# Gate weights of one layer, part of them prepared early beside w_down

## The chip, the cores and the metric

The kernel runs on one core of a Trainium2 chip. The metric is device time in microseconds, the median of several runs. The core's engines each take instructions in their own order: TensorE (PE) for matmuls and transposes, VectorE (DVE), ScalarE (ACT), GpSimd (POOL) and SyncE (SP), which only issues DMAs. GpSimd can issue DMAs too.

## The reference, cut to what matters

One layer for 1,056 tokens (1,024 of a prompt and 32 of a sample) of width 1,024: attention and a gated recurrence in two branches, their mix through w_out, a feed-forward part with a convolution of three tokens, and an input of the layer through a gate. The end, which the change touches:

```python
    ffn = (jax.nn.gelu(ac, approximate=True) * u) @ w_down      # 2816 -> 1024
    x = x + _rms_norm(ffn, g_post_ffn)
    conv_tail = ap[:, ap.shape[1] - (CONV_W - 1):]

    x = x + (pe @ w_ple) * jax.nn.sigmoid(x @ w_ple_gate)       # 1024 -> 1024
    return x, new_k, new_v, s_fin.astype(x.dtype), conv_tail
```

All values are float32.

## The kernel before

A float32 product is made of three matmuls. Each operand is split into a high part, its cast to the matmul's own rounding (fp32r), and a low part, the operand less the high part; the matmuls are high by high, high by low and low by high. The cast is an ACT instruction and the subtraction a DVE instruction (L181 and L184 for plain weights), so each weight tile costs one of both.

The layer's products run one after the other, activations held with features on partitions and tokens along the row. w_up runs as a Strassen-Winograd scheme (L1665 to L1667). Then comes w_down: three groups g of 352 tokens, for each two halves q of 512 output columns, for each half 11 steps of 256 rows of the weight, so 66 steps of 24 matmuls. A step's raw weight (`wr`, 512 KB, two buffers) is loaded by SP, cast to `wh` and split to `wl`; `wh`, `wl` and the gate's parts share one ring of eight tiles (`wb`). After a half, `d_out` copies four banks to `acc`, and sums squares for the norm. `x2_start`, `x2_rows` and `x2_part` finish the norm of a group: sums over partitions and a reciprocal square root on DVE (L211 to L217), transposes of its result into rows on PE (L301), and then `acc` = `acc` times gain times row plus x (L1822, L1823), for each of eight column blocks. For the last group, g = 2, this happens inside the gate stage.

The gate product x @ w_ple_gate comes last. Token groups 0 and 1 are made together by four `gate_unit`s, each with seven products of a Strassen-Winograd scheme, n = 0 to 27, of 12 matmuls each (L2045, L2047, L2048); token group 2 is made by eight plain blocks of 24 matmuls (L200 to L202). The left factors of a unit are seven parts: three quarters of that unit's weight (each 512 rows by 128 columns, 256 KB) and four sums of quarters. Before, SP loads 16 quarters into five buffers (L1885); the four sums of the first unit are made by DVE and those of the other three by GpSimd (L1908 to L1915); every part is then cast by ACT and split by DVE (L1898, L1899). `gate_prepare(n + 3)` asks for parts three products ahead. The right factors, sums of `acc`, are made by `gate_ops` in w_down's last group, with `um` as a buffer.

Behind a product, DVE combines banks into y (L2061 to L2073, U2 and s1c and nU3 in `um`); `y_out` takes tanh on ACT (L1992), multiplies by the loaded `ple` term (L1993, DVE) and adds `acc` (L1994: GpSimd for the gate units, DVE for the plain blocks); `y_done` turns y round by three transposes on PE (L2007), copies it and stores it. `late` holds back y_done until two products later.

The order of instructions on each engine is set when the program is built, by a scheduler that goes by its own estimates of when things are ready; the order of the code is its starting point, and `behind(E)` makes what is in it come after the last instruction written so far for that engine. On the chip each engine and each queue of DMAs goes through its instructions in that order, and a wait holds up what stands behind it.

## Time and profile before

| | |
|---|---|
| median of three runs | 2016.76 us (2016.23 to 2016.99) |
| profiled execution | 2018.78 us, span 2016.6 us |
| mean granted PE clock | 0.997 |
| PE, DVE, ACT, POOL busy | 98%, 73%, 49%, 13% of the span |
| w_down on PE | 1646.5 to 1901.2 us |
| gate units on PE | 1901.4 to 1976.3 us |
| plain blocks on PE | 1976.6 to 2010.2 us |
| HBM traffic | 181.75 MB read, 65.32 MB written |

A row of groups in the profile gives line, engine, operation, written tile <- read tiles, shape and count, then busy time and mean of one in ns, then the idle time of the engine just before and what ended it. A row of waits gives the engine and line that waited, what it waited for, and total, times and longest in us. A row of windows gives the stretch, its length, then busy us and count for PE, its weight loads (PEld), DVE, ACT and POOL, the granted clock, the DMA engines' busy share and GB/s.

### The profile page before, as it was taken

What the parts mean: (1) busy time and instruction counts of PE and PEld (TensorE: products, weight loads), DVE (VectorE), ACT (ScalarE), POOL (GpSimd) and SP (SyncE); (2) the same over time, 40 slices, a digit from 0 to 9 for tenths busy, and PEclk for the clock granted to TensorE, in tenths of its full rate; (3) what the DMA queues carried; (4) which work ended last, traced back from release to release, by engine and by line L of the source; (5) the groups of instructions that cost most, each with busy time, mean ns of one, the idle gap of its engine ahead of it and who ended that gap; (6) DMA issues with size and microseconds to landing.
All of it is one profiled execution on the core that took longest, in us unless ns stands there. A gap on an engine that the chain in (4) does not pass through costs nothing. (4 is left out here: it accounts for less than half of the span.)

```text
span 2016.6 us, 37464 instructions
## 1 busy us (share of the span) xinstructions
PE 1979.0 (98%) x14234; PEld 1946.8 (97%) x14234; DVE 1479.0 (73%) x3249; ACT 985.5 (49%) x2220; POOL 261.8 (13%) x346
## 2 busy tenths in 40 slices
PE   7999999999999999999999999999999999999988
PEld 6999999999999999999999999999999999999988
DVE  6788888688888888553555878787878784647794
ACT  6555566566666666441224663333333344445453
POOL 2110100000000000002001113333333300000140
PEclk9999999999999999999999999999999999999999
DMA  8322311411111111486558572222222255565355
GB/s 265 101 87 82 104 59 53 155 43 58 57 38 53 37 53 53 135 248 205 170 177 275 196 249 84 65 91 69 86 75 80 79 169 199 201 211 180 103 153 151
DMA packets 259257, 249.52 MB, mean 124 GB/s; under 512 B 13621, under 2 KB 227144, under 8 KB 259077
## 3 DMA queue, kind: packets, MB, share of 16 engines
q1 hardware_dynamic: 250533, 219.12, 34.6%
q0 software_dynamic: 8464, 27.94, 3.9%
q8 instruction: 112, 1.84, 0.4%
q14 instruction: 68, 0.56, 0.1%
q10 hardware_dynamic: 80, 0.07, 0.0%
HBM read 181.75 MB, written 65.32 MB: 123 GB/s over the span
## 5 line engine op out<-in xcount | busy, mean ns | idle before, releaser
L1665 PE MATMUL st<-op,wt 128*128 128x264 f32 x1232 | 348.7, 283 | 4.1 <-ACT ple L1420 2.3
L1667 PE MATMUL st<-op,wt 128*128 128x264 f32 x1232 | 350.0, 284 | 0.0
L1666 PE MATMUL st<-op,wt 128*128 128x264 f32 x1232 | 348.2, 283 | 0.0
L184 DVE TENSOR_TENSOR wl<-wr,wh 128x1024 fp32r<-128x1024 f32 x132 | 162.2, 1229 | 118.6 <-ACT wh L181 110.8
L1665 PEld LDWEIGHTS st<-op,wt 128*128 128x128 f32 x1232 | 231.2, 188 | 5.2 <-ACT ple L1420 2.5
L1666 PEld LDWEIGHTS st<-op,wt 128*128 128x128 f32 x1232 | 231.6, 188 | 0.0
L1667 PEld LDWEIGHTS st<-op,wt 128*128 128x128 f32 x1232 | 231.0, 188 | 0.0
L181 ACT CAST wh<-wr 128x1024 fp32r<-128x1024 f32 x116 | 121.8, 1050 | 205.4 <-PE mm L201 135.7
L200 PE MATMUL mm<-ac,wh 128*128 128x352 f32 x528 | 171.0, 324 | 1.7 <-ACT sq L1802 0.9
L1444 ACT CAST wt<-wu 128x512 fp32r<-128x512 f32 x126 | 77.6, 618 | 188.5 <-POOL ab L1651 93.7
L201 PE MATMUL mm<-ac,wh 128*128 128x352 f32 x528 | 169.3, 321 | 0.0
L202 PE MATMUL mm<-ac,wl 128*128 128x352 f32 x528 | 169.2, 321 | 0.0
L200 PE MATMUL mm<-La,wh 128*128 128x384 f32 (+1 forms) x504 | 166.9, 332 | 0.3 <-ACT kt L340 0.3
L201 PE MATMUL mm<-Lb,wh 128*128 128x384 f32 (+1 forms) x504 | 162.8, 323 | 0.0
L202 PE MATMUL mm<-La,wl 128*128 128x384 f32 (+1 forms) x504 | 162.7, 323 | 0.0
L200 PE MATMUL mm<-Ra,wh 128*128 128x264 f32 x512 | 145.7, 285 | 0.0
L201 PE MATMUL mm<-Rb,wh 128*128 128x264 f32 x512 | 145.2, 284 | 0.0
L202 PE MATMUL mm<-Ra,wl 128*128 128x264 f32 x512 | 145.2, 284 | 0.0
L1445 DVE TENSOR_TENSOR wt<-wu,wt 128x512 fp32r<-128x512 f32 x126 | 101.2, 806 | 39.7 <-ACT wt L1444 39.7
L453 ACT ACTIVATE sc<-sc,st 128x257 f32<-128x257 f32 (+1 forms) x144 | 69.7, 485 | 74.9 <-DVE st L448 73.7
L200 PEld LDWEIGHTS mm<-ac,wh 128*128 128x128 f32 x528 | 99.2, 188 | 2.3 <-ACT sq L1802 1.2
L201 PEld LDWEIGHTS mm<-ac,wh 128*128 128x128 f32 x528 | 99.4, 188 | 0.0
(508 smaller groups left out, 5820.3 us busy)
## 6 DMA issues: line engine op xcount, KB each, us to landing
wr<-in_w_down_dram SPq DMA_DIRECT2D x66, 512.0 KB
wu<-in_w_up_dram SPq DMA_DIRECT2D x42, 512.0 KB
wu<-in_w_in_dram SPq DMA_DIRECT2D x32, 512.0 KB
wr<-in_w_in_dram SPq DMA_DIRECT2D x26, 512.0 KB
ac<-act_d SPq DMA_DIRECT2D x66, 176.0 KB
act_d<-Up SPq DMA_DIRECT2D x21, 528.0 KB
wr<-in_w_out_dram SPq DMA_DIRECT2D x16, 512.0 KB
pw_d<-pw POOLq DMA_DIRECT2D x11, 512.0 KB, 5.0
```

The source lines that it names most:

```text
L181: S.copy(hi[:], raw[:])
L184: V.tensor_tensor(lo[:], raw[:], hi[:].bitcast(F32), op=ALU.subtract)
L200: E.matmul(ps, wh, a, start=first and n == 0, stop=False)
L201: E.matmul(ps, wh, b, start=False, stop=False)
L202: E.matmul(ps, wl, a, start=False, stop=last and n == len(ks) - 1)
L453: S.activation(sc[:m_, h, b0:e_ + 1], sc[:m_, h, b0:e_ + 1], AF.Exp, bias=st[:m_, 0, h:h + 1], scale=-1.0, accum_out=st[:m_, 1, h:h + 1])
L1444: S.copy(t[:, 0], src)
L1445: V.tensor_tensor(t[:, 1], src, t[:, 0].bitcast(F32), op=ALU.subtract)
L1665: E.matmul(o, wh, xh, start=first and k == 0, stop=False, skip_group_check=True)
L1666: E.matmul(o, wh, xl, start=False, stop=False, skip_group_check=True)
L1667: E.matmul(o, wl, xh, start=False, stop=k == 3, skip_group_check=True)
```

## The change

A new generator, `gate_early`, is stepped while w_down runs. GpSimd's queue loads the four quarters of a unit into four buffers that are free then: two thirds of `um`, the buffer `wr5` (loaded later, in `gate_first`, before), and two tiles `we` of the ring for outputs. For the first unit, all seven parts are made there, one after the other through a single further tile `we` (`pw`): cast on ACT, store of the high part to DRAM (`pg_d`), subtraction in place on DVE, store of the low part. For the other three units only the sums are made, on DVE, in place, and stored to DRAM (`gs_d`). GpSimd issues these 16 loads and 26 stores of 256 KB.

In the gate stage the first unit's parts are then read from `pg_d`, high and low together, 512 KB each; for the other units `raw_load` reads nine quarters and twelve sums, and cast and split stay there. The y add of L1994 is on DVE for all. GpSimd has no arithmetic there any more. `gate_prepare` asks for four products ahead, `x2_rows(2)` comes at n = 5 behind PE's last instruction instead of at n = 3, `x2_part` at each odd n above 6 behind DVE's last instead of at each n above 4, and `y_done` three products later instead of two, behind PE's last instruction.

```diff
--- before.py
+++ after.py
@@ -124,6 +124,8 @@
     ple_d = dp.tile([P, 8, T], F32, name="ple_d")
     pc_d = [dp.tile([P, 2, 2, H], F32, name=f"pc_d{g}") for g in range(4)]
     act_d = [dp.tile([P, T], F32, name=f"act_d{f}") for f in range(NF)]
+    pg_d = [dp.tile([P, 2, 4, P], F32, name=f"pg_d{i}") for i in range(7)]
+    gs_d = [[dp.tile([P, 4, P], F32, name=f"gs_d{u}_{i}") for i in range(7)] for u in range(4)]
...
@@ -1877,61 +1879,77 @@
 
     quarters, gate_w = [], []
 
-    def quarter_load(n):
-        if n >= 16:
+    def quarter(u, j):
+
+        return rows_cols(w_ple_gate, (j % 2) * 4 * P, (2 * u + j // 2) * P, P, 4)[0]
+
+    extra = ep.tile([P, 4, P], F32R, name="wr5")
+
+    def gate_early():
+        bufs = [um[:, 0:2, :].rearrange("p a c -> p (a c)")[:, 0:512], extra[:].bitcast(F32)]
+        for _ in range(2):
+            t = ep.tile([P, 3, 256], F32, tag="yr", name=nm("we"), bufs=3)
+            bufs.append(t[:].rearrange("p a c -> p (a c)")[:, 0:512])
+        bufs = [b if len(b.shape) == 3 else b.rearrange("p (k c) -> p k c", k=4) for b in bufs]
+        pw = ep.tile([P, 3, 256], F32R, tag="yr", name=nm("we"), bufs=3)
+        pw = pw[:].rearrange("p a c -> p (a c)")[:, 0:512].rearrange("p (k c) -> p k c", k=4)
+        a11, a12, a21, a22 = bufs
+
+        def part(i, src):
+            S.copy(pw, src)
+            gdma(pg_d[i][:, 0], pw.bitcast(F32))
+            V.tensor_tensor(pw, src, pw.bitcast(F32), op=ALU.subtract)
+            gdma(pg_d[i][:, 1], pw.bitcast(F32))
+
+        for u in range(4):
+            for j, b in enumerate(bufs):
+                gdma(b, quarter(u, j))
+            yield
+            if u == 0:
+                for i, b in ((0, a11), (2, a12), (5, a22)):
+                    part(i, b)
+                    yield
+            for o, a, b in ((a22, a21, a22), (a21, a11, a21), (a11, a11, a22), (a12, a12, a11)):
+                V.tensor_tensor(o, a, b, op=ALU.add)
+            if u == 0:
+                for i, b in ((1, a11), (3, a21), (4, a22), (6, a12)):
+                    part(i, b)
+                    yield
+                continue
+            for i, b in ((1, a11), (3, a21), (4, a22), (6, a12)):
+                gdma(gs_d[u][i], b)
+            yield
+
+    def raw_load(n):
+
+        if n >= 28:
             return
-        u, j = divmod(n, 4)
-        c, k0 = ((2 * u, 0), (2 * u + 1, 0), (2 * u + 1, 4), (2 * u, 4))[j]
-        dma(quarters[n % 5], rows_cols(w_ple_gate, k0 * P, c * P, P, 4)[0])
+        u, i = divmod(n, 7)
+        j = {0: 0, 2: 1, 5: 3}.get(i)
+        dma(quarters[n % 5], quarter(u, j) if j is not None else gs_d[u][i])
 
     def gate_first():
         for _ in range(2):
             t = wp.tile([P, 2, 4, P], F32, tag="wr", name=nm("wr"), bufs=2)
             quarters.extend(t[:, i] for i in range(2))
-        quarters.append(ep.tile([P, 4, P], F32, name="wr5")[:])
-        for n in range(5):
-            quarter_load(n)
-
-    def gate_parts():
-        def parts(src):
-            t = part_tile()
-            S.copy(t[:, 0], src)
-            V.tensor_tensor(t[:, 1], src, t[:, 0].bitcast(F32), op=ALU.subtract)
-            gate_w.append(t)
-
-        for u in range(4):
-            n = 4 * u
-            a11, a21, a22, a12 = (quarters[(n + i) % 5] for i in range(4))
-            s1 = wp.tile([P, 4, P], F32, tag="wb", name=nm("sa"), bufs=8)[:]
-            adder = V if u == 0 else G
-            parts(a11)
-            adder.tensor_tensor(s1, a21, a22, op=ALU.add)
-            adder.tensor_tensor(a21, a11, a21, op=ALU.add)
-            adder.tensor_tensor(a11, a11, s1, op=ALU.add)
-            yield
-            parts(a11)
-            yield
-            parts(a12)
-            adder.tensor_tensor(a12, a12, a11, op=ALU.add)
-            quarter_load(n + 5)
-            yield
-            parts(a21)
-            quarter_load(n + 6)
-            yield
-            parts(s1)
-            yield
-            parts(a22)
-            quarter_load(n + 7)
-            yield
-            parts(a12)
-            quarter_load(n + 8)
-            yield
-
-    gate_gen, op_gen = gate_parts(), gate_ops()
+        quarters.append(extra[:].bitcast(F32))
+        for n in range(7, 12):
+            raw_load(n)
 
     def gate_prepare(n):
         while len(gate_w) < min(n + 1, 28):
-            next(gate_gen)
+            i = len(gate_w)
+            t = part_tile()
+            if i < 7:
+                dma(t[:].bitcast(F32), pg_d[i][:])
+            else:
+                src = quarters[i % 5]
+                S.copy(t[:, 0], src)
+                V.tensor_tensor(t[:, 1], src, t[:, 0].bitcast(F32), op=ALU.subtract)
+                raw_load(i + 5)
+            gate_w.append(t)
+
+    op_gen, early_gen = gate_ops(), gate_early()
 
...
@@ -1967,9 +1985,12 @@
                     op_steps({18: 1, 20: 1}.get(k, 0) if q == 0 else
                              {0: 1, 2: 2, 4: 1, 6: 1, 8: 1, 12: 1, 14: 2, 16: 1, 18: 1, 20: 1}.get(k, 0))
                     if q and k == 18:
+                        gate_prepare(2)
+                    if q and k == 20:
                         gate_first()
-                    if q and k == 20:
-                        gate_prepare(3)
+                        gate_prepare(4)
+                if g == 1:
+                    next(early_gen, None)
 
...
@@ -1981,7 +2002,6 @@
 
     def y_out(g, c, b, y=None):
 
-        adder = V if y is None else G
...
@@ -1991,7 +2011,7 @@
         for z_ in cols:
             S.activation(y[:, z_], b[:, z_], AF.Tanh, scale=0.5)
             V.scalar_tensor_tensor(y[:, z_], y[:, z_], 1.0, pl[:, z_], op0=ALU.add, op1=ALU.mult)
-            adder.tensor_tensor(y[:, z_], y[:, z_], a[:, z_], op=ALU.add)
+            V.tensor_tensor(y[:, z_], y[:, z_], a[:, z_], op=ALU.add)
         return y
 
...
@@ -2034,7 +2054,7 @@
         for i, (t, first) in enumerate(((x, True), (y, True), (x, False), (y, False), (zz, True),
                                         (y, False), (zz, False))):
             n = 7 * u + i
-            gate_prepare(n + 3)
+            gate_prepare(n + 4)
...
@@ -2048,10 +2068,12 @@
                 E.matmul(t, w[:, 1, k, :], a, start=False, stop=k == 3, skip_group_check=True)
             if n == 1:
                 x2_start(2)
-            if n == 3:
-                x2_rows(2)
-            if n > 4:
-                x2_part()
+            if n == 5:
+                with behind(E):
+                    x2_rows(2)
+            if n > 6 and n % 2:
+                with behind(V):
+                    x2_part()
...
@@ -2072,8 +2094,9 @@
             else:
                 V.tensor_tensor(r, U2, zz, op=ALU.add)
                 late.append((n, 1, c, y_out(1, c, r, r)))
-            while late and late[0][0] + 2 <= n:
-                y_done(*late.pop(0)[1:])
+            while late and late[0][0] + 3 <= n:
+                with behind(E):
+                    y_done(*late.pop(0)[1:])
 
```

Line numbers from there on are larger by two in the changed kernel, and by some twenty from `y_out` on: L181, L301, L1796 and L1994 before are L183, L303, L1798 and L2014 after.

ScalarE in w_down's first group, before: casts of weights (`wh`), one of an activation pair (`ac`), and the first copies of a finished half.

```order
L181 CAST wh_20182<-wr_20180 128x1024
L1756 CAST ac_19998<-ac_19999 128x704
L181 CAST wh_20212<-wr_20210 128x1024
L181 CAST wh_20242<-wr_20240 128x1024
L181 CAST wh_20272<-wr_20270 128x1024
L181 CAST wh_20302<-wr_20300 128x1024
L181 CAST wh_20332<-wr_20330 128x1024
```

The same place after; `we_20849` is the tile through which all seven parts go. The first row shown belongs to w_down's seventh step.

```order
L183 CAST wh_20188<-wr_20186 128x1024
L1899 CAST we_20849<-um 128x512
L183 CAST wh_20218<-wr_20216 128x1024
L1758 CAST ac_20033<-ac_20034 128x704
L183 CAST wh_20248<-wr_20246 128x1024
L1899 CAST we_20849<-wr_20057 128x512
L183 CAST wh_20278<-wr_20276 128x1024
L183 CAST wh_20308<-wr_20306 128x1024
L1899 CAST we_20849<-we_20848 128x512
```

A cast of a part now stands between the casts of weights, about every second step from the seventh to the eighteenth; DVE's subtractions of parts stand between its splits in the same way.

GpSimd's queue at that place, after; before, it had nothing there between w_up and the gate stage.

```order
L1900 DMA pg_d_162<-we_20849 128x512
L1902 DMA pg_d_162<-we_20849 128x512
L1900 DMA pg_d_165<-we_20849 128x512
L1902 DMA pg_d_165<-we_20849 128x512
L1900 DMA pg_d_161<-we_20849 128x512
L1902 DMA pg_d_161<-we_20849 128x512
L1906 DMA um<-in_w_ple_gate_dram 128x4x128
```

The stores of the high and the low part of each product alternate, and the next unit's loads stand among them.

TensorE in the gate units, product n = 4, before: the norm's transposes (L301) come after its first two matmuls.

```order
L2045 MATMUL mm_22440<-gx_21954,wt_22454 128x352
L2047 MATMUL mm_22440<-gx_21954,wt_22454 128x352
L301 MATMUL tr_22531<-ident,nr_22471 128x128 x2
L301 MATMUL tr_22531<-ident,nr_22471 128x96
L2048 MATMUL mm_22440<-gx_21954,wt_22454 128x352
```

After, with the end of product n = 5 and the beginning of n = 6:

```order
L2067 MATMUL mm_22540<-gx_22155,wt_22555 128x352
L2068 MATMUL mm_22540<-gx_22155,wt_22555 128x352
L303 MATMUL tr_22669<-ident,nr_22571 128x128 x2
L303 MATMUL tr_22669<-ident,nr_22571 128x96
L2027 MATMUL tr_22682<-ident,y_22606 128x128 x2
L2027 MATMUL tr_22682<-ident,y_22606 96x128
L2065 MATMUL mm_22541<-gx_22462,wt_22592 128x352
```

The norm's transposes have moved 22 matmuls later, and the first y's transposes, which stood ten matmuls behind them, now stand right after them.

## The prediction

> **What bounds the kernel now.** I read the page first, then TensorE's waits, then the last 110 us in pieces.
>
> ```profile
> PE 1979.0 (98%) x14234; PEld 1946.8 (97%) x14234; DVE 1479.0 (73%) x3249; ACT 985.5 (49%) x2220; POOL 261.8 (13%) x346
> POOL 2110100000000000002001113333333300000140
> ```
>
> PE is busy for 98% of the span, so a change that keeps the same matmuls can only win in the 2% in which PE stands still or runs slowly, and can lose wherever it makes PE wait. GpSimd (POOL) works in w_up (the 3s), then rests, and works again in two slices near the end: the gate units, where this change strikes.
>
> ```profile
> PE tr L2007 <- POOL y L1994: 5.4, 5, 2.3
> PE tr L301 <- DVE nr L217: 3.9, 1, 3.9
> PE mm L200 <- DVE Sp L1694: 0.9, 1, 0.9
> PE tr L2007 <- DVE y L1994: 0.9, 1, 0.9
> 1901.20:1966.20 65.00, 54.83 (x326) 51.81 (x324) 55.23 (x91) 31.16 (x76) 32.14 (x24) 0.95 0.46 134
> 1966.20:2010.40 44.20, 44.15 (x287) 43.70 (x287) 20.05 (x30) 16.28 (x41) 3.79 (x4) 1.00 0.56 164
> ```
>
> The waits (total, times, longest) put the second and third largest at the transposes of y, behind GpSimd's add, and at the norm rows, behind a chain on DVE. The windows (busy PE, PEld, DVE, ACT, POOL; clock; DMA share) show where: from 1901.2 to 1966.2 PE is idle for 10.2 of 65.0 us, and afterwards for nothing. In that stretch DVE is busy for 55.2 us, which is 85%.
>
> Idle time is not the whole loss, because matmuls after a gap run slower:
>
> ```profile
> 1901.37 0.41 PE L2045 MATMUL mm<-gx,wt 128*128 128x352 f32 x1
> 1914.17 1.59 PE L301 MATMUL tr<-ident,nr 128*128 128x128 f32 x6 [3.94 <-DVE nr L217]
> 1916.20 0.50 PE L2047 MATMUL mm<-gx,wt 128*128 128x352 f32 x1
> 1916.50 0.50 PE L2048 MATMUL mm<-gx,wt 128*128 128x352 f32 x1
> 1976.16 0.33 PE L2048 MATMUL mm<-gx,wt 128*128 128x352 f32 x1
> 1976.57 0.41 PE L200 MATMUL mm<-gx,wh 128*128 128x352 f32 x1
> 1976.82 0.33 PE L201 MATMUL mm<-gx,wh 128*128 128x352 f32 x1
> 2008.75 0.32 PE L200 MATMUL mm<-gx,wh 128*128 128x352 f32 x1
> 2010.02 0.33 PE L202 MATMUL mm<-gx,wl 128*128 128x352 f32 x1
> 2010.19 0.49 PE L2007 MATMUL tr<-ident,y 128*128 128x128 f32 x3
> 1910.00:1915.00 5.00, 1.06 (x6) 0.83 (x5) 4.79 (x13) 0.56 (x1) 2.60 (x2) 0.88 0.13 36
> 1915.00:1920.00 5.00, 5.00 (x28) 4.98 (x28) 3.44 (x8) 2.30 (x6) 0.00 (x0) 0.78 0.58 180
> 1930.00:1935.00 5.00, 5.00 (x24) 5.00 (x23) 5.00 (x10) 2.55 (x7) 1.45 (x1) 0.66 0.86 240
> ```
>
> From 2008.75 to 2010.02 lie eight gaps between matmul starts, 0.16 us each; after the 3.94 us wait the starts are 0.30 apart, and the granted clock of the slices after gaps is 0.78 and 0.66. I price the stage by content: from its first matmul (1901.37) to the first of the two last transposes (2010.19) are 108.8 us. In it are 336 matmuls of the gate units and 192 of the plain blocks, 528 x 0.16 = 84.5 us. A group of three transposes between matmuls costs 1976.82 - 1976.16 - 2 x 0.16 = 0.34 us; 22 of them are 7.5 us. Some 1.5 us go to the norm's other transposes and sums at full clock. That makes 93.5, so about **15 us are lost**: 10 idle, 5 slow clock and restarts. The 3.94 us wait costs 5.7 of them with its slow matmuls. The Trainium skill ("TensorE: Matmul & The Clock Gate", section "What's actually happening") has the clock halve after an idle window of about 3.4 us. By it only the 3.94 us gap would cost clock and the stake would be about 1.4 us smaller; the trace disagrees, since its 0.66 slice follows a gap of 2.34 us.
>
> **The gate stage, part by part.** These rows stand beside GpSimd's work, but for the last three, which come from quiet stretches or stages:
>
> ```profile
> L1899 DVE TENSOR_TENSOR wt<-wr,wt 128x512 fp32r<-128x512 f32 x19 | 17.0, 904 | 4.8 <-ACT wt L1898 4.8
> L1993 DVE SCALAR_TENSOR_TENSOR y<-y,pl 128x352 f32<-128x352 f32 x12 | 9.5, 792 | 1.0 <-ACT y L1992 0.9
> L216 DVE TENSOR_TENSOR rst<-rst,nv 128x3 f32<-128x3 f32 x3 | 1.5, 502 | 0.1
> L1994 POOL TENSOR_TENSOR y<-y,acc 128x352 f32<-128x352 f32 x12 | 14.8, 1230 | 20.2 <-DVE y L1993 17.1 <-DVE nr L217 3.2
> 1908.84 0.69 DVE L1899 TENSOR_TENSOR wt<-wr,wt 128x512 fp32r<-128x512 f32 x1 [2.59 <-ACT wt L1898]
> 1909.95 0.62 ACT L1898 CAST wt<-wr 128x512 fp32r<-128x512 f32 x1 [0.27 <-PE mm L2048]
> L1803 DVE TENSOR_TENSOR sqd<-sqd,sq 128x352 f32<-128x352 f32 x6 | 3.1, 524 | 1.7 <-ACT sq L1802 1.5
> ```
>
> Removed: twelve sums and sixteen y adds on GpSimd. Added on DVE here: the sixteen y adds, 16 x 0.52 = 8.3 us. Taken from DVE here: the stretching beside GpSimd, 19 x (0.90 - 0.69) + 12 x (0.79 - 0.52) = 7.2 us of these two groups, and about 5 more of the small ops and the norm's (L216 takes a mean of 502 ns for 3 columns). So DVE has about 51 us of work instead of 55, for a PE that wants the stretch done in 50: DVE is now almost as long as PE. That is the weak place.
>
> Each y loses 1.23 - 0.52 = 0.7 us of its chain and gets one part (twelve matmuls, 1.9 us) more time before its transposes: 2.6 us together, more than the longest wait there, 2.3. The norm rows stand 22 matmuls later (3.5 us) and their chain is no longer stretched: the 3.94 us wait goes, and with it 5.7. Parts are prepared four ahead instead of three, with seven of them read ready-made as one 512 KB load; the loads are issued as tiles come free in w_down's last steps, and I cost them at nothing; cover is two parts, 3.8 us. If that fails, PE waits for each.
>
> What is late next is DVE: with 51 us in 50 it falls a little behind whenever two results come together. PE's new stalls lie between 0 and half of the stake (7.5 us); I take 3.5, nearer the middle since both ends of the chain got slack. Gate stage: -15.0 + 3.5 = **-11.5**.
>
> **The w_down part.** What moves there is 16 loads on GpSimd's queue, seven casts, seven splits, sixteen sums (four for each unit), and 26 stores. PE does 24 matmuls for a step, 24 x 0.16 = 3.82 us, and is never idle there.
>
> ```profile
> L184 DVE TENSOR_TENSOR wl<-wr,wh 128x1024 fp32r<-128x1024 f32 x28 | 34.3, 1225 | 33.8 <-ACT wh L181 30.9 <-PE mm L202 2.6
> L181 ACT CAST wh<-wr 128x1024 fp32r<-128x1024 f32 x28 | 29.4, 1050 | 46.2 <-PE mm L201 36.7 <-DMA wr<-in_w_down_dram 8.9 <-DVE ac L1757 0.6
> t_d<-hs POOLq DMA_DIRECT2D x16, 192.0 KB, 2.3
> mx_d<-ta POOLq DMA_DIRECT2D x32, 132.0 KB, 3.3
> pw_d<-pw POOLq DMA_DIRECT2D x11, 512.0 KB, 5.0
> 1670.00:1680.00 10.00, 10.00 (x65) 10.00 (x64) 4.28 (x4) 3.15 (x3) 0.00 (x0) 1.00 0.50 177
> 1710.00:1720.00 10.00, 10.00 (x65) 10.00 (x64) 5.46 (x6) 5.29 (x6) 0.00 (x0) 1.00 0.75 249
> 1730.00:1740.00 10.00, 10.00 (x67) 10.00 (x66) 7.19 (x10) 5.94 (x13) 0.00 (x0) 1.00 0.79 268
> ```
>
> The engines have room: the sixteen sums and seven splits are 23 x 0.69 = 16 us on a DVE about half busy. The order is the danger. All seven parts share one tile: cast, store of the high half, split in place (which waits until that store has landed), store of the low half, and only then the next cast. The waiting split holds DVE's queue and the waiting cast holds ACT's, and behind each stand w_down's own splits and casts. The order gives the six rounds between first and seventh cast eleven weight steps, 11 x 3.82 = 42 us, 7.0 us for a round. A round takes 0.62 + 0.69 + two landings. A 256 KB store was not run before; between 192 KB at 2.3 us and 512 KB at 5.0 a straight line gives 2.84, an estimate, and 132 KB at 3.3 says that it may be more. With 2.84 and some 0.3 us of hand-overs a round is 7.3 us, a slip of 6 x 0.3 = 1.8 us over all. Against that stands the lead: the weight ring's eight tiles hold four steps, casts wait for PE to free one (36.7 us in the row), so weights are ready about three steps less cast and split ahead: 11.4 - 2.6 = 8.8 us. A slip of 1.8 stays under it, and I cost the rounds at **0**. Bounds: 0, and with landings of 5.0 a round of 11.6 us, 27.6 us of slip, 18.8 after the lead.
>
> Traffic: 42 x 256 KB = 10.5 MB. At 249 GB/s for a share of 0.75 the full rate is 332 GB/s. Between 1670 and 1742 the share is about 0.6, so 9 MB fit; the other 1.5 MB push what runs there by up to 4.5 us, again under the lead: 0. One load goes ahead of w_down's first operands, where PE already waits 0.9 us; 256 KB at the full rate is **+0.8**.
>
> The Trainium skill ("SBUF — State Buffer", section "SBUF: two separate sides") speaks against this part: transfers issued from GpSimd's queue need descriptors that GpSimd writes, and it cannot while DVE holds the shared port. The rows that could show it are only the landings above; what they would mean is the first rival.
>
> Sum: -11.5 + 0.8 = -10.7 us. The profiled execution took 2018.78 us for a span of 2016.6, 2.0 us over the median of 2016.76; I take the difference from the median: **2006.0 us**.
>
> **The rivals.**
>
> *Store round trips hold w_down.* Place: the splits and casts between weight steps 7 and 18. For it: the pw_d stores' median of 5.0 us, on the same queue, beside a busy DVE. Against it: t_d's 2.3, nearly the size, and that pw_d is twice the size. At 5.0 the time is 2006.0 + 18.8 = 2024.8. The gain is used up when the slip is 8.8 + 10.7 = 19.5 us, a round of 10.25, a landing of 4.3; the kernel is slower by over 0.2% from a landing of 4.7.
>
> *DVE becomes the bound in the gate units.* With the busy share of 85% that it had, 51 us take 60 instead of 65, and the slow clock stays partly: a gain of 5 to 7, about 2011. If waits for ACT and PE take more, to 75%, 51 us take 68 and nothing is gained: 2018. For it: 85% is already high and the y adds come on top; against it: much of DVE's idle time before came from waits on GpSimd's chain.
>
> *Both halves middling.* Landings near 3.5 give a round of 8.6 and a slip of 9.6, just past the lead; with saturated queues behind it some 5 us of PE waits: 2012.
>
> **How the numbers follow.** What a measurement can tell from no change is about 0.2%, 4 us. Forecast 0.45, its own range 2001.8 (all 15 us won) to 2010; both halves middling or DVE at 85%, still faster, 0.20; the same cases at their bad ends, within 0.2%, 0.15; round trips, slower, 0.20. Faster 0.65, same 0.15, slower 0.20. The range leaves out the slower case: 2001.5 to 2020.5.
>
> **What the profile after would show.** PE's waits for POOL y and for nr gone; in the 75 us of gate units no slice with a clock under 0.9; GpSimd with no arithmetic there; the splits of the gate weights (L1899 before) near 0.65 us instead of 0.90. Landings of pg_d under 3.5 us and no PE wait between 1646 and 1901. Wrong would make it: a wait of PE for wh or wl there, splits waiting for pg_d, or DVE busy above 95% with PE waiting for it.

## The result, and the profile after

The changed kernel takes 2033.9 us (median of six runs) against 2017.7 for the kernel before: slower by 0.75% (ratio 1.0075, 95% interval 1.0060 to 1.0089). The forecast was 0.5% faster.

From the page after: busy time of the engines, and PE's busy share and its granted clock (PEclk) in tenths over 40 slices.

```profile
span 2031.9 us, 37557 instructions
...
PE 1984.7 (98%) x14234; PEld 1952.9 (96%) x14234; DVE 1478.2 (73%) x3277; ACT 986.9 (49%) x2220; POOL 252.3 (12%) x360
...
PE   8999999999999999999999999999999998799998
...
PEclk9999999999999999999999999999999999899999
```

PE has a hole in the 34th and 35th slice, about 1680 to 1780, where before it had none, and the 39th, in the gate units, is a 9 where it was an 8. The waits of PE after, total, times and longest, over the whole execution:

```profile
PE mm L202 <- ACT sq L1804: 9.5, 1, 9.5
...
PE mm L204 <- DVE wl L186: 4.7, 2, 3.4
PE mm L202 <- ACT sqd L1801: 4.3, 1, 4.3
...
PE mm L202 <- DVE Sp L1696: 1.3, 1, 1.3
```

And from the first gate matmul to the end of the execution, the whole list (the shorter of the two waits for y, 0.9 us, comes after the last gate matmul):

```profile
PE tr L2027 <- DVE y L2014: 2.0, 2, 1.1
PE mm L2065 <- DVE um L2083: 0.8, 1, 0.8
PE mm L2065 <- DVE y L2089: 0.4, 1, 0.4
PE mm L2065 <- ACT um L2081: 0.3, 1, 0.3
```

The waits for GpSimd's y and for the norm rows are gone. In their place PE waits in w_down: for split weights (wl), and much more for the copies that empty a half's four banks, the buffers into which PE adds up its products (L1804 and L1801 stand behind the copies, in `d_out`). The stretches (us, then busy PE, PEld, DVE, ACT, POOL, clock, DMA share, GB/s):

```profile
1690.00:1700.00 10.00, 4.43 (x21) 3.85 (x20) 8.09 (x11) 4.32 (x9) 2.37 (x4) 0.82 0.53 176
...
1730.00:1740.00 10.00, 6.57 (x34) 6.28 (x33) 5.26 (x7) 3.89 (x5) 2.37 (x4) 0.87 0.92 295
...
1750.00:1760.00 10.00, 2.17 (x7) 2.18 (x8) 5.16 (x7) 6.22 (x13) 1.86 (x3) 0.55 0.99 333
...
1940.00:1945.00 5.00, 5.00 (x36) 5.00 (x36) 4.97 (x11) 3.01 (x7) 0.00 (x0) 1.00 0.65 203
...
1955.00:1960.00 5.00, 5.00 (x34) 4.98 (x34) 5.00 (x12) 3.07 (x8) 0.00 (x0) 1.00 0.83 252
```

From the first matmul of w_down to the first of the gate units, and from there to the end of the last gate matmul, in the two profiled executions (w_down begins at 1644.5 us before; the 1646.5 of the table at the start is behind its first wait):

| kernel | w_down us | PE idle in it | gate stage us | PE idle in it |
|---|---|---|---|---|
| before | 256.9 | 1.7 | 109.0 | 10.2 |
| after | 281.6 | 19.8 | 97.3 | 2.7 |
| difference | +24.7 | +18.1 | -11.7 | -7.5 |

The gate stage won what was forecast, and w_down lost twice as much: 18.1 us more of idle PE and 6.6 more of busy PE, for the same matmuls. Behind the 9.5 us wait, for one, matmuls start 0.29 us apart for 3 us and 0.16 from then on. How far a wait goes is seen on ScalarE before the longest hole:

```profile
1743.45 1.05 ACT L183 CAST wh<-wr 128x1024 fp32r<-128x1024 f32 x1 [4.08 <-DVE we L1913]
1744.75 1.05 ACT L183 CAST wh<-wr 128x1024 fp32r<-128x1024 f32 x1 [0.25 <-DMA wr<-in_w_down_dram]
1752.59 0.78 ACT L1758 CAST ac<-ac 128x704 fp32r<-128x704 f32 x1 [6.78 <-DMA ac<-act_d]
1753.28 1.04 ACT L183 CAST wh<-wr 128x1024 fp32r<-128x1024 f32 x1
1755.44 1.61 ACT L1758 CAST ac<-ac 128x704 fp32r<-128x704 f32 x2 [1.13 <-DMA ac<-act_d]
1756.96 0.45 ACT L1798 COPY acc<-mm 128x352 f32<-128x352 f32 x1
```

A cast of weights waits 4.1 us for a sum of gate quarters (DVE, L1913); a cast of activations two places behind it waits 6.8 us for its load; the copies of the banks stand behind both, and PE stands from 1748.3 to 1757.8.

### The profile page after: what moved, and what is told of

It reads as the page before. It is cut to its first block, busy times and chain, and to the rows that moved or that the text cites. A ratio compares the mean times of both kernels' runs of the same rounds, so it can differ in the third digit from the quotient of the medians.

```text
span 2031.9 us, 37557 instructions
## 1 busy us (share of the span) xinstructions
PE 1984.7 (98%) x14234; PEld 1952.9 (96%) x14234; DVE 1478.2 (73%) x3277; ACT 986.9 (49%) x2220; POOL 252.3 (12%) x360
## 5 line engine op out<-in xcount | busy, mean ns | idle before, releaser
L183 ACT CAST wh<-wr 128x1024 fp32r<-128x1024 f32 x116 | 121.8, 1050 | 202.8 <-PE mm L203 126.3
L202 PE MATMUL mm<-ac,wh 128*128 128x352 f32 x528 | 173.6, 329 | 15.9 <-ACT sq L1804 9.5
L203 PE MATMUL mm<-ac,wh 128*128 128x352 f32 x528 | 171.3, 325 | 0.0
L202 PEld LDWEIGHTS mm<-ac,wh 128*128 128x128 f32 x528 | 100.9, 191 | 17.0 <-ACT sq L1804 9.8
L204 PEld LDWEIGHTS mm<-ac,wl 128*128 128x128 f32 x528 | 100.8, 191 | 5.3 <-DVE wl L186 5.3
```

The lines of the kernel that those rows point to most:

```text
L183: S.copy(hi[:], raw[:])
L202: E.matmul(ps, wh, a, start=first and n == 0, stop=False)
L203: E.matmul(ps, wh, b, start=False, stop=False)
L204: E.matmul(ps, wl, a, start=False, stop=last and n == len(ks) - 1)
```

## The experiments

What was open was which of three things makes the loss: the rounds of part, store, subtraction and store through one tile (R); sums that wait for quarters, which are loaded only after stores have landed (Q); or the transfers themselves (T). Each ratio below is against runs of the kernel before on the same chip. Since the time at which w_down begins varies from run to run by up to 8 us (1644 to 1652 in these profiles, whatever the kernel), the two stages' own lengths are the better measure. Each is from one profiled execution: w_down, where nothing was changed in it (before, no early work, and the three runs on the gate stage further down), took 255.7 to 256.9 us, so about 1 us between two rows says nothing.

| run | ratio (95%) | w_down us | idle | gate us | idle |
|---|---|---|---|---|---|
| no early work | 0.9942 (0.9925 to 0.9960) | 255.9 | 1.0 | 99.2 | 4.0 |
| parts alone | 1.0043 (1.0030 to 1.0055) | 274.1 | 11.2 | 97.2 | 2.3 |
| sums alone | 1.0001 (0.9990 to 1.0011) | 268.6 | 10.0 | 98.5 | 3.6 |
| spread out | 1.0039 (1.0023 to 1.0054) | 273.4 | 13.0 | 98.2 | 3.1 |
| copies first | 1.0103 (1.0079 to 1.0127) | 285.7 | 21.2 | 96.7 | 1.9 |
| spread out, copies first | 1.0054 (1.0037 to 1.0071) | 272.7 | 11.8 | 96.9 | 2.1 |
| the same, no wait for stores | 1.0039 (1.0026 to 1.0053) | 274.5 | 12.6 | 98.0 | 3.1 |
| away from activation loads | 1.0044 (1.0030 to 1.0057) | 276.1 | 14.6 | 97.9 | 3.1 |
| transfers alone | 1.0016 (1.0006 to 1.0027) | 270.4 | 10.3 | 96.6 | 1.8 |
| transfers alone, even | 0.9992 (0.9979 to 1.0004) | 269.1 | 8.9 | 97.9 | 3.0 |
| later order alone | 0.9998 (0.9986 to 1.0009) | 256.2 | 1.3 | 108.6 | 9.5 |
| y adds on DVE alone | 0.9990 (0.9978 to 1.0002) | 255.8 | 0.9 | 109.5 | 11.2 |
| later order and y adds | 0.9972 (0.9957 to 0.9986) | 255.7 | 0.7 | 106.4 | 8.0 |
| late sums | 0.9965 (0.9951 to 0.9979) | 262.9 | 4.4 | 96.1 | 1.7 |
| late sums, wider | 0.9965 (0.9952 to 0.9979) | 257.8 | 1.0 | 104.3 | 6.9 |
| the same, norm later | 0.9983 (0.9974 to 0.9992) | 257.0 | 1.9 | 102.6 | 6.4 |

**No early work.** The step of the generator is left out, and the loads of the gate stage read other data of the same size.

```diff
-        dma(quarters[n % 5], quarter(u, j) if j is not None else gs_d[u][i])
+        dma(quarters[n % 5], quarter(u, 2 if j is None else j))
...
-                dma(t[:].bitcast(F32), pg_d[i][:])
+                dma(t[:].bitcast(F32), pw_d[i][:].rearrange("p (a k c) -> p a k c", a=2, k=4))
...
-                if g == 1:
-                    next(early_gen, None)
```

> Everything of the change but the work beside w_down: gate_early is left out, so the gate stage reads other data of the same size (pw_d for pg_d, whole quarters for the sums of gs_d) and its result is not the gate's. If the whole loss sits in w_down, its 66 steps take 255 us again as before and the gate stage the 97 us that it takes after: 2017 - 11.8, about 2005.5 us. If part of the loss belongs to the gate stage's new loads, over 2012.

Its median is 2007.8 us, w_down is 255.9 us and the gate stage 99.2. The whole loss is the early work beside w_down: without it, and with all the new loads of the gate stage, the kernel is faster than before by 0.58%.

**Parts alone, sums alone.** The generator's loop runs over the first unit only, or over the other three. What is not made is replaced in the gate stage by loads of other data. In sums alone the generator is stepped at the steps 12 to 21 of w_down, where the sums stand in the change.

```diff
-        for u in range(4):
+        for u in range(1):        # parts alone; sums alone: range(1, 4)
```

> Only the first unit's parts are made beside w_down, through the one shared tile; the sums of the units 1 to 3 are left out (the gate stage reads whole quarters in their place, so its result is wrong). Theory R, the rounds of cast, store, subtraction and store through one tile hold the queues of DVE and ACT: the PE waits around 1690 to 1698 (1.3 and 4.3 us) stay, with their slow clock and the start 9 us over no early work, about 2014. If R were the whole loss: 2030. Theory Q, the loss is the sums' waits for their loads: about 2006.

> Only the sums of the units 1 to 3 are made beside w_down, at the steps at which they stand in the change; the first unit's parts are left out (the gate stage reads pw_d instead, so its result is wrong). Theory Q, sums wait on DVE for quarters that are loaded only after the previous unit's stores have landed: PE waits of 3.4 and 9.5 us near 1735 and 1750 with slow clock, about 17 us over no early work, 2022. Theory R: about 2006, since no part goes through the shared tile.

Parts alone lose 18.2 us of w_down against no early work, sums alone 12.7, both together 25.7. Neither half of the work is the loss by itself, and R is worth twice what was expected here. The two do not add up: together they lose 5.2 us less than the sum of 30.9. If each had first to use up one common reserve, together they would lose more than the sum, so a shared reserve is not what this shows. In parts alone PE's waits at the banks are these:

```profile
PE mm L202 <- ACT sq L1804: 6.0, 1, 6.0
PE mm L202 <- ACT sqd L1801: 3.9, 1, 3.9
```

The 3.9 us come in the step behind weight step 11, where the second half begins; the 6.0 come in the step behind 22, some 15 us after the last store of a part was issued. In sums alone the only long wait stands at that second place:

```profile
PE mm L202 <- ACT sq L1804: 8.7, 1, 8.7
```

No sum waits for a quarter in this run, neither on DVE nor, through DVE, on ScalarE. So Q as it was meant did not happen there, and 12.7 us were lost all the same. What grew are ScalarE's waits for loads of weights: 52.6 us between 1645 and 1900, where they are 27.6 without early work.

**Spread out.** All the early work, a step of it behind the weights of every third step of w_down.

```diff
-                if g == 1:
-                    next(early_gen, None)
+                steps[0] += 1
+                if 3 <= steps[0] <= 45 and steps[0] % 3 == 0:
+                    with behind(V, S):
+                        next(early_gen, None)
```

> The whole change with its stores, loads, parts and sums, but each step of gate_early is queued on DVE and ACT behind the weights of every third step of w_down, from the first group on, so that parts and sums are spread over 45 steps instead of 20. Theories R and Q (queue order): nothing waits, w_down takes 255 to 257 us again, about 2006. Theory T, the 10.5 MB of added traffic itself makes weights late or holds DVE: the same bytes are moved, so w_down stays 10 us or more too long, 2017 or more.

With 9 to 25 us from one part's cast to the next, w_down still loses 17.5 us, so crowding is not the whole of it. DVE still waits 12.5 us for stores of parts here, so R is not out yet.

**Copies first.** If PE waits for banks although weights lie ready (theory B), it should help to queue the next casts behind the copies. That was done in the change and in the spread-out version.

```diff
-                w = next_w()
+                if k < 4 and (g or q):
+                    with behind(S):
+                        w = next_w()
+                else:
+                    w = next_w()
...
-                    load_chunk(g + 1, i)
+                    if k == NF - 2:
+                        with behind(S):
+                            load_chunk(g + 1, i)
+                    else:
+                        load_chunk(g + 1, i)
```

> The whole change, and at the end of each half of w_down ScalarE's casts of the next weights and activations are queued behind the copies that empty the half's banks, not ahead of them. Theory B, a delay of ScalarE's queue reaches PE through the banks, whose copies stand behind casts for steps two and three ahead, long before the weights run out: the PE waits for the copies (4.3 and 9.5 us in the change) go and with them their slow clock; the waits for split weights (4.7 us) stay or grow a little: about 2017. If the weights themselves are late by as much (theory R or Q without B), PE waits for weights instead: 2030 or more.

> The spread-out version of the whole change (a step of the early work every third step of w_down) with the casts behind the copies at each half's end. Theory B: the delays that were left there (2 to 3.5 us for a subtraction that waits for its store) are under the lead of the weights, PE waits for no copies, about 2009, the time without early work plus 1 to 2. Theory T, the traffic makes weights late: 2020 or more.

Theory B falls as a cure: the change gets slower by 4 us of w_down. PE now waits more for weights, and 7.5 us for copies stay:

```profile
PE mm L204 <- DVE wl L186: 8.1, 4, 6.4
PE mm L202 <- ACT sq L1804: 7.5, 1, 7.5
PE mm L202 <- ACT wh L183: 2.8, 1, 2.8
```

The spread-out version stays as it was, within 1 us. The banks are where the delay is seen first, but putting them first does not take it away; ScalarE itself is late.

**No wait for stores, and away from the activation loads.** The low part goes to two free pieces of 256 columns, so the subtraction waits for no store; the first kernel is otherwise the spread-out version with copies first. The second leaves casts and copies in the change's order and queues the work at steps that were meant to have no loads of activations.

```diff
-            V.tensor_tensor(pw, src, pw.bitcast(F32), op=ALU.subtract)
-            gdma(pg_d[i][:, 1], pw.bitcast(F32))
+            for z in range(2):
+                V.tensor_tensor(lo[z].bitcast(F32R), src[:, 2 * z:2 * z + 2, :],
+                                pw[:, 2 * z:2 * z + 2, :].bitcast(F32), op=ALU.subtract)
+            for z in range(2):
+                gdma(pg_d[i][:, 1, 2 * z:2 * z + 2, :], lo[z])
...
+                if steps[0] in (5, 7, 9, 11, 25, 26, 28, 29, 30, 31, 32, 34, 35, 37):
```

> As the spread-out version with copies first, and the low parts go to two free pieces of 256 columns instead of back into the shared tile, so that no subtraction waits for a store. Theory R: the last waits of DVE for stores go and the time is that without early work, 2008; theory T as before 2020 or more. If the waits of DVE no longer matter once the copies stand first, the same time as the spread-out version with copies first.

> The whole change, its early work placed only at steps of w_down without activation loads (parts at steps 10 to 14 and 29 to 33, sums from 28 to 40), the low parts in two free pieces so that no subtraction waits for its store. Theory T1, the added traffic does harm where the next group's activations are loaded (steps 18 to 27 and 40 to 49), since the two buffers of raw weights have no slack left there: no PE wait for copies at the end of steps 22 and 44, about 2009. Theory T2, any 10 MB added to w_down delay weights until PE waits: still 2020 or more.

In the first, neither ScalarE nor DVE waits for the early work at all, and w_down still loses 18.6 us against no early work. What ScalarE waits for between 1645 and 1900, and for comparison the same three rows of the kernel before below it:

```profile
ACT wh L183 <- DMA wr<-in_w_down_dram: 83.4, 38, 7.0
ACT ac L1758 <- DMA ac<-act_d: 36.9, 18, 5.6
ACT wh L183 <- PE mm L203: 10.6, 6, 2.8
```

```profile
ACT wh L181 <- PE mm L201: 67.1, 28, 3.1
ACT wh L181 <- DMA wr<-in_w_down_dram: 29.8, 17, 3.2
ACT ac L1756 <- DMA ac<-act_d: 18.5, 6, 4.5
```

Before, casts wait mostly for PE to free the ring: weights are ahead. Now they wait for their loads. The second run was to test T1, harm only beside activation loads, and it does not settle it. W_down takes 276.1 us, and PE waits 2.1 and 1.9 us behind the steps 11 and 33, with no activation loads near: as the whole loss T1 falls. But the last 12 of its 49 transfers were issued from 1798 to 1817, around activation loads from 1802 on, and the longer waits follow there: 4.4 us in step 40, behind a sum that waited 6.9 us for its quarter, and 5.0 behind step 44.

**Transfers alone.** The 42 DMAs without casts, subtractions and sums, first every second step in bursts, then about one for a step. The diff is of the first; a write of one column on DVE sets the pace.

```diff
-            for o, a, b in ((a22, a21, a22), (a21, a11, a21), (a11, a11, a22), (a12, a12, a11)):
-                V.tensor_tensor(o, a, b, op=ALU.add)
+                V.memset(b[:, 0, 0:1], 0.0)      # ahead of each load, and of each store of unit 0
```

> Only the DMAs of the early work, 42 of 256 KB each, every second step of w_down, with no cast, no subtraction and no sum (what is stored is the plain quarter, so the result is wrong); a write of one column on DVE sets the pace. Theory T, the added 10.5 MB alone makes loads late: over 2020. Theories R and Q with B, the waits of DVE and ACT for these transfers do the harm: no queue waits here, about 2009 to 2012.

> Only the 42 early DMAs, about one for each of 42 steps of w_down, with no cast, subtraction or sum (the result is wrong); a write of one column on DVE before each sets the pace. Theory T1, only bursts on top of the activation loads make weights late: 256 KB in 3.8 us is 69 GB/s beside some 200 of 332, no PE wait, about 2009. Theory T2, each early transfer in flight lengthens a weight load (4.0 us alone, 4.5 to 6 beside early transfers in the runs so far) beyond the 1.3 us of slack that two raw buffers leave: w_down 265 us or more, 2016 to 2022.

They lose 14.5 and 13.2 us of w_down: a little over half of the change's 25.7. In the first, DVE still waited 13 us for stores at its writes of one column; in the second 4.6 us in all for loads and stores, and the loss is nearly the same. In the second, PE waits for copies again, twice:

```profile
PE mm L202 <- ACT sq L1804: 7.9, 2, 4.4
PE mm L202 <- DVE Sp L1696: 1.0, 1, 1.0
```

The two long waits, 4.4 and 3.5 us, stand behind the steps 22 and 44, the two turns between groups, where SP loads the next group's activations and ScalarE casts them before the copies; at the turns inside a group there is none. (In bursts 2.5 us stand behind step 22 and 6.5 behind 33, inside a group.) The kernel before has its one wait for copies, 0.9 us, behind step 44 too.

ScalarE's waits for loads of weights between 1645 and 1900, 27.6 us without early work, are 65.1 and 50.2. What a transfer does is seen in the time of a weight load, from SP's issue to the landing. It is known only for loads that a cast waited for, so these are the late ones (mean, count). The right half has other loads of SP within some 5 us (activations, and x for the norm); where exactly that line is drawn moves a few loads between columns, and the means of the last by up to 1 us:

| run | alone | beside early transfers | with SP's other loads | with both |
|---|---|---|---|---|
| before | 4.0 (9) | | 4.5 (8) | |
| no early work | 4.0 (7) | | 4.7 (11) | |
| after | 3.8 (4) | 4.4 (8) | 4.4 (4) | 6.1 (4) |
| transfers alone | 4.1 (6) | 5.6 (12) | 4.3 (6) | 5.9 (6) |
| the same, even | 4.3 (3) | 4.3 (13) | 5.1 (1) | 5.7 (7) |
| no wait for stores | 3.9 (10) | 4.5 (16) | 4.1 (5) | 6.8 (7) |

A raw buffer is used again every second step, 7.63 us, and cast and split take 1.05 + 1.23 = 2.28 of these, so a load may take 5.3. At 4.0 it gives back 1.3 us for two steps; at 5.7 to 6.8 each load takes 0.4 to 1.5 us of the lead. The sign fits. Load by load, what lies above 5.35 us adds up to 14.0 us in transfers alone, 5.1 when they are even and 14.3 with no wait for stores, and to 0.1 or less before and without early work. The losses are 14.5, 13.2 and 18.6, so this sum does not give the loss, least of all when the transfers are even. How the rest reaches PE is open. So is whether it matters that GpSimd's queue carries the transfers: no run issued them from another.

**The gate stage's gain.** Parts of the change made in the kernel before: the later order (first diff), the y adds on DVE (second), and both.

```diff
-            if n == 3:
-                x2_rows(2)
-            if n > 4:
-                x2_part()
+            if n == 5:
+                with behind(E):
+                    x2_rows(2)
+            if n > 6 and n % 2:
+                with behind(V):
+                    x2_part()
...
-            while late and late[0][0] + 2 <= n:
-                y_done(*late.pop(0)[1:])
+            while late and late[0][0] + 3 <= n:
+                with behind(E):
+                    y_done(*late.pop(0)[1:])
```

```diff
-        adder = V if y is None else G
+        adder = V
```

> The kernel before with the later order of the gate stage alone: the norm's rows at n = 5, x2 parts behind at odd n, y_done three products later; sums and y adds stay on GpSimd, nothing is made early. Theory L, the later transposes make the gain of the gate stage (12 us with everything): 8 to 10 us faster than before. Theory G, the gain comes from GpSimd leaving DVE alone: at most 3 us faster, the waits move.

> The kernel before with the y adds of the gate units on DVE and nothing else; the sums stay on GpSimd. Theory G: 5 us or more faster than before, PE's waits for y and for the norm rows shrink. Theory L: within 3 us of before, since the norm rows' wait of 3.9 us stays and DVE gets 8 us more work.

> Both: the later order and the y adds on DVE, with the sums still on GpSimd and no early work. If the parts read from DRAM matter little for the gate stage, this wins nearly all of its 12 us without the traffic beside w_down: 2008 to 2010. If the sums on GpSimd and their waits matter, 2013 or more.

Theories L (the later order) and G (GpSimd leaving DVE alone) both fall as single causes. With the later order the waits for nr and for y's transposes go, and as many come at the banks, for DVE (later order alone, then both):

```profile
PE mm L2045 <- DVE um L2067: 5.5, 2, 2.8
PE mm L2045 <- DVE um L2063: 4.0, 2, 2.5
PE tr L2007 <- ACT yr L2021: 0.9, 1, 0.9
```

```profile
PE mm L2045 <- DVE um L2067: 4.5, 3, 2.3
PE mm L2045 <- DVE um L2063: 3.3, 2, 1.8
PE tr L2007 <- DVE y L1994: 0.9, 1, 0.9
```

Together they win 2.6 of the gate stage's 11.7 us, and either alone nothing beyond the 1 us between rows. The other 9 come with what else the change does there: GpSimd's sums leave, the first unit's parts are read ready-made, and parts are asked for four products ahead. The late sums further down do without the second of these; no run separates the other two. In "both", DVE's instructions still take longer than after the change (a split of the gate weights in "both", then after; count, busy, mean ns):

```profile
L1899 DVE TENSOR_TENSOR wt<-wr,wt 128x512 fp32r<-128x512 f32 x19 | 14.1, 742 | 4.3 <-ACT wt L1898 4.3
```

```profile
L1948 DVE TENSOR_TENSOR wt<-wr,wt 128x512 fp32r<-128x512 f32 x21 | 14.4, 685 | 1.2 <-ACT wt L1947 1.1
L2013 DVE SCALAR_TENSOR_TENSOR y<-y,pl 128x352 f32<-128x352 f32 x18 | 9.4, 520 | 3.4 <-ACT y L2012 3.4
```

The Trainium skill ("SBUF — State Buffer", section "SBUF: two separate sides") has the port pair that DVE and GpSimd share locked by whichever starts first, when GpSimd reads SBUF and DVE has two inputs there. The rows agree in that a split takes 720 to 904 ns in the four kernels in which GpSimd has arithmetic in the stage, and 685 where it has none. They do not follow how much it has: 904 before and 759 with the later order alone, both with sums and y adds on GpSimd; 720 with the y adds on DVE, and 742 with both. Its other rule, that transfers issued by GpSimd starve while DVE holds that pair, no run here shows or rules out: the issues of the parts' stores took 540 to 559 ns.

**Late sums.** A version for the finding: only the sums of units 1 to 3 are made early, in w_down's last group, where no activations are loaded any more; the first unit's parts are made at w_down's end from its quarters, its sums on DVE. The gate stage keeps the changed order. The diff shows the main lines.

```diff
-        for u in range(4):
+        for u in range(1, 4):
...
-                if g == 1:
-                    next(early_gen, None)
+                steps[0] += 1
+                if steps[0] in (45, 48, 50, 53, 55, 58):      # wider: (45, 50, 51, 54, 55, 59)
+                    with behind(V):
+                        next(early_gen, None)
...
-                dma(t[:].bitcast(F32), pg_d[i][:])
+                next(zero)
```

> A correct version with less early work, and later: only the sums of the units 1 to 3 are made early, in w_down's last group (steps 50 to 63, no activation loads there), 24 DMAs; the first unit's parts are made from its quarters at w_down's end as before, its sums on DVE; the gate stage's order is the changed one. Theory T1: w_down stays within 3 us of 256, the gate stage takes 97 to 102: 2009 to 2013, faster than both. Theory T2: w_down 262 to 266, about 2017 to 2020.

> As the version with late sums, the three units' sums four to five steps apart and further behind their loads (steps 53 to 63 instead of 50 to 63). If the 7.9 us wait of a sum for its quarter made the rest of the loss, w_down takes 258 or less and the time falls by another 3 to 5 us, to 0.5% or 0.6% under before. If the transfers alone make it, w_down stays at 261 to 264 and the ratio at 0.9965.

The first is faster than both kernels: 2014.0 us, ratio 0.9965 (0.9951 to 0.9979), with a gate stage of 96.1. Its first unit's parts are not read ready-made, so the gate stage's gain does not need that. In w_down DVE waits once for long for a quarter:

```profile
DVE we L1900 <- DMA we<-in_w_ple_gate_dram: 7.9, 1, 7.9
```

With the sums further behind their loads w_down is 257.8 us, with all 24 transfers still in it: 2 us over no early work. But the gate stage then has, 9 us after its start, a wait of 5.1 us of PE's sums over partitions for DVE's sums of squares (`sqd`), it takes 104.3, and the time stays. Moving the norm behind that:

```diff
-            if n == 1:
-                x2_start(2)
-            if n == 5:
+            if n == 3:
+                with behind(E):
+                    x2_start(2)
+            if n == 6:
```

> As the version with sums further behind their loads, and the norm's sums over partitions come after the product n = 3 instead of n = 1 on PE, the norm's rows after n = 6 instead of n = 5. If the 5.1 us wait of PE for the sums of squares is all that keeps the gate stage at 104, it goes to 99 or 100: 2010, 0.55% under before. If DVE is simply behind by that much, the wait moves to the next transposes and nothing is gained.

The wait moved, as the second reading had it: 4.0 us for ScalarE's `um` at nearly the same time, gate stage 102.6. DVE and ScalarE are behind at the turn from w_down to the gate. Why they are not in the first version is open. Over both stages the three versions take 359.0, 362.1 and 359.6 us, where no early work takes 355.1 and the kernel before 365.9. So the late sums, with the first unit's parts back at the turn, still cost 4 to 7 us; they are only far cheaper than the early ones.

## Why the prediction was wrong

**"Gate stage: -15.0 + 3.5 = -11.5": right in size.** It was -11.7, PE's waits for POOL y and for nr are gone, no slice is under a clock of 0.9, GpSimd has no arithmetic there, the splits take 685 ns, and PE's waits that are left are 2.7 us where 3.5 of time were allowed for stalls. Wrong was the reason given for single waits: that a y with 2.6 us more time and rows 22 matmuls later win them. That order alone won 0.4 us and with the y adds 2.6; PE then waits for DVE at the banks instead. The other 9 us came with the sums' leaving, which also ends GpSimd's stretching of DVE, and with parts asked for four ahead. That these help because DVE is the stage's second bound fits the rows, and is not shown by itself. That the number came out within 0.2 us is in part luck.

**"The other 1.5 MB push what runs there by up to 4.5 us, again under the lead: 0": the step that failed most.** The transfers alone cost 13 to 14.5 us, also when spread evenly. I had summed bytes over 72 us against the full rate. With the even transfers the DMA engines are busy for 0.78 of the time from 1660 to 1840, against 0.61 before: far from full, and yet 13.2 us are lost. Such a sum does not see that a single weight load takes longer, 4.0 us alone and 5.7 to 6.8 beside early transfers and SP's other loads, in a pipeline of two raw buffers that allows 5.3; how much of the loss that makes is not settled.

**"I cost the rounds at 0": mis-sized.** The view of the parts' stores:

```profile
L1900 POOL DMA_DIRECT2D pg_d<-we x7: 540/540/559, 1664.7 to 1719.8; - x7
...
who waited for it (us, times):
  DVE we L1901: 19.6, 5
  ACT we L1899: 14.8, 5
...
DMA to landing us min/median/max: 2.3/3.1/7.2
```

The median landing, 3.1, is near the 2.84 of the sum, but a chain of rounds pays the mean. The twelve landings of the six rounds take 42.5 us, 3.5 each, and the first store 7.2. The six rounds took 55.1 us, 9.2 for a round where 7.3 had been worked out: that is 13 us of slip, not 1.8. Some 8.5 of the 11.3 us between these two are longer landings, and the rest is hand-overs, 0.8 us a round where 0.3 was taken. The sign of being wrong that was named, splits waiting for `pg_d`, is in the view: 19.6 us. Parts alone cost 18.2 us.

**"Weights are ready about three steps less cast and split ahead, 8.8 us": wrong as a cover.** It was held against the rounds and against the traffic, 1.8 and 4.5 us, which it would have covered even together. The sizes were wrong, and so was what it covers. In parts alone, where the slip is 13.9 us, a lead of 8.8 would leave 5.1 to lose, and 18.2 were lost. What PE needs first when a new half begins is banks, whose copies stand on ScalarE behind casts for later steps and behind activations, and 13.8 of the 18.5 us that PE waits for copies or split weights are there.

**"256 KB at the full rate is +0.8": about right.** At w_down's first operands PE waited 0.9 and 1.3 us, where it waited 0.9 before; parts alone and sums alone, with the same load ahead, have 0.4 and 1.3.

**The first rival** had the place, the sign and the size of a loss (18.8 us) and a chance of 0.20; its condition, a landing of 5.0, did not hold, so the near size is luck. **The third rival** had the condition that came, landings near 3.5, and saturated queues beside them; it gave the two together some 6 us. The loss of 25.7 came as the rounds, waits for quarters and slower loads together; the runs do not part it exactly.

**DVE as the bound in the gate units** did not come: in the stretch from 1940 to 1960 it is busy for 18.4 of 20 us, and PE for all of it.

## What to carry to other kernels

In a stage that keeps PE busy for 99% and moves its weights through two buffers, a free share of bandwidth is not enough to go by: compare also the time of one load, as casts wait for it, with two steps less the work on it, before putting other transfers beside it. A chain of round trips pays their mean, not their median. Before a lead is taken for a cover, look for what PE needs first at each turn (here banks, not weights). Work that leaves a crowded stage needs a place where it can wait: the sums of three units, with 24 transfers, cost w_down 12.7 us beside its first group and the start of the second, and 1 to 7 us in its last, where no activations are loaded.

## What the runs showed of the hardware that was not expected

Of the loads of 512 KB that a cast waited for, those alone took 3.8 to 4.3 us in the mean of a run, those beside 256 KB pieces on GpSimd's queue 4.3 to 5.6, and those with SP's other loads as well 5.7 to 6.8 (3 to 16 loads each). Loads and stores of the same size on GpSimd's queue differ much after the change (median time to landing at the end):

```profile
pg_d<-we POOLq DMA_DIRECT2D x14, 256.0 KB, 3.1
...
we<-in_w_ple_gate_dram POOLq DMA_DIRECT2D x8, 256.0 KB, 5.8
```

But this is not a property of loads and stores: with the transfers alone, in bursts, the same `we` loads took 5.5 us and the stores of `pg_d` from `we` 5.8, and from one tile (`um`) loads took 4.0 and stores 5.8 to 6.0. So the time of such a transfer is no constant, and which of the two takes longer changed with the way they were issued.

And a wait of PE costs more than its length: of w_down's 24.7 us of loss 6.6 are longer busy time for the same matmuls, with a granted clock of 0.55 in the slice with the 9.5 us wait.
